# Hybrid attention trunk on one core: rotary embedding kept in PSUM, differential attention steps and a norm load moved, weight residuals emitted in pieces

## The chip, the cores and the metric

The kernel runs on one core of one Trainium2 chip. The time is the device time of one execution in microseconds, as the median of several runs. The core's engines are named as in the profile: PE is TensorE (PEld its weight loads), DVE is VectorE, ACT is ScalarE, POOL is GpSimd, and SP is SyncE, which here does nothing but issue DMAs.

## What is computed

Two layers over an input of 512 rows and 1024 columns, all in fp32. Each layer normalises its input, maps it by one input projection to three groups of heads, runs differential attention (a), stick-breaking attention (b) and forgetting attention (c), gates each with a SiLU path, maps the concatenation back, normalises and adds. Cut to what matters here:

```
h = rms_norm(x, g_pre)
qa, ka, va, ga, qs, ks, vs, gs, qf, kf, vf, gf, ff = split(h @ w_in)
qa, ka = rope(qa), rope(ka)              # first 16 of each 64 head dims
ya = rms_norm((softmax(q0 k0) - lam * softmax(q1 k1)) @ va, sub_gain) * silu(ga)
yb = stick_breaking(qs, ks, vs) * silu(gs)
yc = softmax(qf kf + forget bias) @ vf * silu(gf)
x  = x + rms_norm(concat(ya, yb, yc) @ w_out, g_post)
```

## The kernel before

Every operand of the projections is split in a high part (rounded to the matmul's type, `F32R`) and a low part (the rest), and `mm3` (L191 to L194) adds three matmuls per block: high x high, high x low, low x high.

Weights come in "halves" (`add_in_unit`, `add_out_unit`): tiles of 128 x 4 x 256 of `w_in`, or 128 x 2 x 512 of `w_out`. `load_to` (L162) issues the load of a half into one of three `raw` buffers on the SP queue. `split_to` (L170) makes the high part by a copy on ACT (L176), and the low part by subtractions of 256 columns on POOL (L182, four in a row for a half), or on DVE (L185) where the half is marked `lo="dve"` or in part `"both"`. Right after the split it issues the load of the third half ahead (L189), which needs the buffer of the half just split.

The order of all work is a plan. `do(cost, fn)` puts PE's projection work in a row and moves the plan's clock on; `at(t, fn)` puts other work at a time of that clock, in nanoseconds. At the end everything is sorted by that time and emitted (L850 to L852). Each engine runs its own instructions in that order, and an instruction that waits holds up all behind it on its engine. A tile's buffer is handed on when all that read it is done.

A half that is used at time t is split at t less its `lead` (2500 to 10833), and never later than the halves after it: `limit = min(limit, t - lead)` in L843 to L846.

One layer in the order of PE: values of group a, queries and keys of group a (four units of 256 columns for q and k, each of two projections of 24 matmuls of 512 columns), then values, queries and keys of group c, with the attention steps of group a between them, then group b with the steps of c, then the three gates with the steps of b, then the output projection in two passes of 512 columns. A projection's result lies in one of three PSUM buffers `pj` (L80).

The places that the change touches:
- `rope_stages` (L299): for each q and k projection of group a, DVE shuffles the result out of PSUM (L303, tile `sh`), multiplies it by the cosine table into an SBUF tile `ra` (L305), multiplies `sh` by the sine table (L306) and adds both into `ra` (L307). `qk_done` then makes high parts on ACT (L319) and low parts on DVE (L324) from `ra`; for groups b and c, which have no rope, from `pj` itself.
- `step_a` (L375): one step of differential attention (16 in a layer, a head and 128 queries each): two score matmuls into the two `s` buffers (L357), the masked minimum `mn` on DVE (L364), exponentials on ACT (L373), combination on DVE, transposes on PE, the product with the values (`av`, with the tile `on`, L402) and, 17029 after the step's start, `back` (L415). L629 places the steps: they start 3518 after the start of group c, over a span of 50075.
- `step_c`: `diag` (L456) on POOL adds the causal mask to the bias tile (`cm`) ahead of each score.
- The pre-norm of the next layer (L235 to L249): the mean and its power -0.5 stand on POOL (L242, L245), then DVE scales (L248) and PE transposes (L254).
- The output projection's first pass has six halves with low parts on POOL, the second six with low parts on DVE. At the end of the first pass DVE multiplies each accumulator by the post-norm gain (`y`, L756); the second pass takes over those `pj` buffers. `new_post` (L761) loads that gain, 9000 before the end of the first pass (L765).

Of the kernel before, what the change touches and what calls it, by code (L numbers as in the profile page):

```python
# [10 lines left out]
F32 = mybir.dt.float32  # L11
# [3 lines left out]
ALU = mybir.AluOpType  # L15
# [9 lines left out]
UW = 256  # L25
# [35 lines left out]
def hybrid_kernel(ctx, tc, x, w_in, forget_bias, diff_lambda, diff_subln, w_out, pre_norm, post_norm, consts, out):  # L61
    nc = tc.nc
# [26 lines left out]
    C = {}  # L89
# [30 lines left out]
    def t2(name, shape=None):  # L120
        return t2_p.tile(shape or [128, S], F32, name=name, tag="t2")
# [10 lines left out]
    now = [0.0]  # L132
# [5 lines left out]
    def at(t, fn):  # L138
        side.append((t, 0, len(side), fn))


    halves = []
    st_load = [0]
    st_split = [0]

    def add_in_unit(l, c0, extra=None):
        w = UW + (8 if extra is not None else 0)
        k0 = len(halves)
        for h in range(2):
            rows = w_in[l, h * 512:(h + 1) * 512]  # L150
            src = [(rows[:, c0:c0 + UW].rearrange("(k p) c -> p k c", p=128), 0, UW)]
            if extra is not None:
                src.append((rows[:, extra:extra + 8].rearrange("(k p) c -> p k c", p=128), UW, w))
            halves.append(dict(src=src, shape=[4, w], pool=whl_p, tag="whl", lead=9500 if h == 0 else 8000))
        return k0
# [6 lines left out]
    def load_to(k):  # L162
        while st_load[0] < min(k, len(halves)):
            h = halves[st_load[0]]
            h["raw"] = raw_p.tile([128] + h["shape"], F32, name="raw", tag="raw")
            for src, lo, hi in h["src"]:
                nc.sync.dma_start(out=h["raw"][:, :, lo:hi], in_=src)
            st_load[0] += 1

    def split_to(k):  # L170
        while st_split[0] < min(k, len(halves)):
            h = halves[st_split[0]]
            load_to(st_split[0] + 1)
            raw = h.pop("raw")
            hl = h["pool"].tile([128, 2] + h["shape"], F32R, name="hl", tag=h["tag"])
            nc.scalar.activation(out=hl[:, 0], in_=raw, func=AF.Copy)  # L176
            n = h["shape"][0]
            m = {"dve": 0, "both": n // 2}.get(h.get("lo"), n)
            for k in range(m):
                for c in range(0, h["shape"][1] // UW * UW, UW):  # L180
                    e = h["shape"][1] if c + 2 * UW > h["shape"][1] else c + UW
                    nc.gpsimd.tensor_tensor(out=hl[:, 1, k, c:e], in0=raw[:, k, c:e], in1=hl[:, 0, k, c:e].bitcast(F32),  # L182
                                            op=ALU.subtract)
            if m < n:
                nc.vector.tensor_tensor(out=hl[:, 1, m:n], in0=raw[:, m:n], in1=hl[:, 0, m:n].bitcast(F32),  # L185
                                        op=ALU.subtract)
            h["hl"] = hl
            st_split[0] += 1
            load_to(st_split[0] + 3)  # L189

    def mm3(ps, lh, ll, rh, rl, first, last):  # L191
        nc.tensor.matmul(out=ps, lhsT=lh, rhs=rh, start=first, stop=False)  # L192
# [106 lines left out]
    def rope_stages(st, scale):  # L299
        def turn():  # L300
            ps = st["ps"]
            sh = t2("sh")
            nc.vector.stream_shuffle(out=sh, in_=ps, mask=swap)  # L303
            ra = t2("ra")
            nc.vector.scalar_tensor_tensor(out=ra, in0=ps, scalar=scale, in1=C["rope"][:, 0], op0=ALU.mult, op1=ALU.mult)  # L305
            nc.vector.scalar_tensor_tensor(out=sh, in0=sh, scalar=scale, in1=C["rope"][:, 1], op0=ALU.mult, op1=ALU.mult)  # L306
            nc.vector.tensor_tensor(out=ra, in0=ra, in1=sh, op=ALU.add)  # L307
            st["ps"] = ra

        return [(0, turn)]  # L310

# [241 lines left out]
    def steps(fn, c, t0, span, w=W_STEP):  # L553
        t = t0
        for p in range(4):
            for i in range(NT):
                fn(t, c, p, i)
                t += span / 16 * w[i]
# [3 lines left out]
    def use(k, t):  # L562
        uses.append((k, t))
# [43 lines left out]
    def plan_layer(l, L):  # L607
# [9 lines left out]
        for g in ("a", "c", "b"):  # L617
            base = G[g]
            c = dict(pairs=[{} for _ in range(4)], lc=lc)
            st = {}  # L620
            c["v"] = lambda st=st: st["v"]
            c["o"] = lambda st=st: st["o"]
            c["cs"] = cs[l]
            t0 = now[0]
            at(t0, lambda st=st: st.update(v=v_p.tile([128, NT, 512], F32, name="v", tag="v")))
            if prev is not None:
                pst, pc, pg = prev
                at(t0, lambda pst=pst: pst.update(o=o_p.tile([128, 4, S], F32, name="o" + pg, tag="o")))
                steps(step_a if pg == "a" else step_c, pc, t0 + (3518 if pg == "a" else 3191), 50075 if pg == "a" else 46774)  # L629
            order = [(u, tt) for u in range(2) for tt in range(NT)]  # L630
            if g == "a":
                order = [(0, 0), (0, 1), (0, 2), (1, 0), (1, 1), (1, 2), (0, 3), (1, 3)]
            ks = []
            for u in range(2):
                ks.append(add_in_unit(l, base + 1024 + u * UW, 6144 if g == "a" and u == 0 else None))
            seen = set()
            for u, tt in order:
                ex = g == "a" and u == 0
                w = UW + (8 if ex else 0)
                if u not in seen:  # L640
                    seen.add(u)
                    use(ks[u], now[0])
                    use(ks[u] + 1, now[0] + 1300)
                    if g == "a" and u == 1:
                        halves[ks[u]]["lead"], halves[ks[u] + 1]["lead"] = 7500, 6500

                def done(pst, u=u, tt=tt, ex=ex, st=st, w=w):
                    def ev():
                        nc.scalar.activation(out=st["v"][:, tt, u * UW:(u + 1) * UW], in_=pst["ps"][:, 0:UW],
                                             func=AF.Copy)  # L650
                        if ex:
                            if "ff" not in ffd:
                                ffd["ff"] = lay.tile([128, 32], F32, name="ff", tag="ff")
                            nc.vector.tensor_copy(ffd["ff"][:, tt * 8:(tt + 1) * 8], pst["ps"][:, UW:w])
                    return [(0, ev)]
                proj_N(ks[u], w, tt, hT, done)
            if g == "a":
                at(now[0] + 2000, lambda: layer_consts(lcd, l))
                at(now[0] + 5000, lambda: ffd.update(lf=decay(ffd["ff"], lcd, l)))
                at(now[0] + 9000, lambda: decay_sum(ffd["lf"], l))  # L660
            sc = 0.125 if g == "b" else -0.125
            for u in range(2):
                for part in ("q", "k"):
                    k0 = add_in_unit(l, base + u * UW + (512 if part == "k" else 0))
                    use(k0, now[0])
                    use(k0 + 1, now[0] + 2600)
                    if g == "a" and u == 0 and part == "q":
                        for h in range(2):
                            halves[k0 + h].update(lead=2500, lo="both")
                    for cc in range(2):  # L670
                        keep = c["pairs"][2 * u + cc]
                        if part == "q":
                            proj_T(k0, cc, hT, lambda pst, keep=keep: qk_done(pst, g == "a", sc, keep, "q"))
                        else:
                            proj_T(k0, cc, hT, lambda pst, keep=keep: qk_done(pst, g == "a", 1.0, keep, "k"))
            prev = (st, c, g)
            ctxs[g] = (st, c)

        t0 = now[0]
# [55 lines left out]
        for u, (g, j0) in enumerate(order):  # L735
            k = add_out_unit(l, row[g] + j0, 0, whl_p, "whl")
# [24 lines left out]
        def new_post():  # L761
            t = qk_p.tile([128, 2, S], F32, name="gain", tag="qs")
            gains["post"] = [t[:, 0], t[:, 1]]
            load_gain(gains["post"], post_norm[l])
        at(now[0] - 9000, new_post)  # L765
        N = None
        if l + 1 < DEPTH:
            nx = {}
# [8 lines left out]
        for u, (g, j0) in enumerate(order):  # L777
            k = add_out_unit(l, row[g] + j0, 1, *((o_p, "o") if u < 3 else (v_p, "v") if u == 3 else (whl_p, "whl")))
# [3 lines left out]
        for tt in range(NT):  # L782
            sl = slice(tt * 128, (tt + 1) * 128)
            st = {}
# [54 lines left out]
    FIRST_LO = {0: "both", 1: "both"}  # L839
    first_norm(L)  # L840
    for l in range(DEPTH):
        L = plan_layer(l, L)
    limit = float("inf")  # L843
    for k, t in reversed(uses):
        limit = FIRST_SPLIT.get(k, min(limit, t - halves[k]["lead"]))
        at(limit, lambda k=k: split_to(k + 1))  # L846

    for k, e in FIRST_LO.items():
        halves[k]["lo"] = e
    with tc.manual_schedule():  # L850
        for _, _, _, fn in sorted(main + side, key=lambda e: e[:3]):
            fn()  # L852
# [28 lines left out]
```

## Time and profile before

| | us |
|---|---|
| time, median of 3 runs | 873.25 (873.04 to 873.48) |
| profiled execution | 873.66 |
| its span | 871.8 |
| PE busy | 854.9 |
| DVE, ACT, POOL busy | 495.3, 476.9, 449.6 |

The span runs from the first to the last instruction of the program on the core; the time of the execution has 1.9 us around it. The profile's rows tell for a group of equal instructions the busy time and the mean of one, and in a timeline the start, the length and, in brackets, for how long the engine stood idle before it and what ended that.

### The profile page before, as it was taken

To read this page: it belongs to the slowest core of one execution; us is meant where nothing else is said; L and a number is where in the kernel's file an instruction comes from. 1 tells how busy PE (TensorE), PEld (TensorE's weight loads), DVE (VectorE), ACT (ScalarE), POOL (GpSimd) and SP (SyncE) were. 2 spreads that over 40 slices of the span, in tenths; PEclk is the share of its full clock that TensorE was granted. 3 is DMA by queue.
4 is the path that set the end of the run, shared out by engine and by line. 5 is a ranking of instruction groups with operands and counts; after the bars stand their busy time and mean duration, and the time that the engine had idled before them with its cause. 6 is when DMAs were issued, how large, how long until landed. Compare 5 with 4: busy or idle time off the path is not lost.

```text
span 871.8 us, 13938 instructions
## 1 busy us (share of the span) xinstructions
PE 854.9 (98%) x4892; PEld 721.4 (83%) x4892; DVE 495.3 (57%) x1143; ACT 476.9 (55%) x1064; POOL 449.6 (52%) x680
## 2 busy tenths in 40 slices
PE   7999999999999999999999999999999999999997
PEld 5988998898778778777898889888987787877885
DVE  5378656544565778623563875664445476774322
ACT  4344667766776556633334356676667756664310
POOL 4366554655444548770364664555554544688301
PEclk9999999999999999999999999999999999999999
DMA  7365323432524221237264452325335422122522
GB/s 233 89 164 138 96 73 98 117 102 76 154 67 116 75 72 49 73 107 257 78 177 114 123 145 74 99 72 146 97 81 137 106 66 72 49 78 92 164 101 97
DMA packets 73207, 94.27 MB, mean 108 GB/s; under 512 B 6433, under 2 KB 56225, under 8 KB 73138
## 3 DMA queue, kind: packets, MB, share of 16 engines
q1 hardware_dynamic: 70834, 89.19, 35.6%
q10 hardware_dynamic: 2304, 4.20, 1.5%
q8 instruction: 39, 0.64, 0.3%
q14 instruction: 30, 0.25, 0.1%
HBM read 76.56 MB, written 4.23 MB: 93 GB/s over the span
## 4 chain that ended last, share of the span: by engine, by line
PE 78%; DVE 10%; ACT 4%; POOL 3%; issue 2%; DMA 2%; DVEq 0%; POOLq 0%; ACTq 0%; SPq 0%
PE pj L192 18%; PE pj L194 18%; PE pj L193 17%; PE s L339 6%; PE pt L347 5%; PE ov L437 4%; POOL hl L182 2%; PE acc L192 2%; PE acc L193 2%; PE acc L194 2%; PE ov L399 2%; DVE ra L307 2%; DVE sh L306 2%; DVE sh L303 1%; DVE qd L324 1%
## 5 line engine op out<-in xcount | busy, mean ns | idle before, releaser
L182 POOL TENSOR_TENSOR hl<-raw,hl 128x256 fp32r<-128x256 f32 (+1 forms) x420 | 343.5, 850 | 237.1 <-ACT hl L176 213.0
L192 PE MATMUL pj<-hT,hl 128*128 128x512 f32 x576 | 236.6, 411 | 0.0
L194 PE MATMUL pj<-hT,hl 128*128 128x512 f32 x576 | 225.7, 392 | 0.0
L193 PE MATMUL pj<-hT,hl 128*128 128x512 f32 x576 | 225.3, 391 | 0.0
L176 ACT ACTIVATE hl<-raw 128x1024 fp32r<-128x1024 f32 (+1 forms) x120 | 126.3, 1058 | 35.4 <-DMA raw<-in_w_out_dram 18.9
L194 PEld LDWEIGHTS pj<-hT,hl 128*128 128x128 f32 x576 | 108.1, 188 | 24.3
L192 PEld LDWEIGHTS pj<-hT,hl 128*128 128x128 f32 x576 | 108.4, 188 | 20.0 <-issue 2.1
L193 PEld LDWEIGHTS pj<-hT,hl 128*128 128x128 f32 x576 | 108.7, 189 | 16.9
L192 PE MATMUL pj<-hl,hT 128*128 128x256 f32 (+1 forms) x384 | 112.2, 292 | 0.3 <-ACT hT L257 0.2
L194 PE MATMUL pj<-hl,hT 128*128 128x256 f32 (+1 forms) x384 | 109.5, 285 | 0.5 <-DVE hT L258 0.5
L193 PE MATMUL pj<-hl,hT 128*128 128x256 f32 (+1 forms) x384 | 109.3, 285 | 0.5 <-POOL hl L182 0.5
L373 ACT ACTIVATE p<-p,mn 128x128 f32<-128x128 f32 (+3 forms) x128 | 71.1, 556 | 33.6 <-DVE mn L364 31.7
L506 DVE TENSOR_TENSOR_SCAN kp<-kp,c_masks 128x128 f32<-128x128 f32 (+3 forms) x64 | 67.2, 1051 | 18.3 <-ACT kp L499 17.8
L192 PEld LDWEIGHTS pj<-hl,hT 128*128 128x128 f32 x384 | 73.7, 192 | 1.3 <-ACT hT L257 1.0
L193 PEld LDWEIGHTS pj<-hl,hT 128*128 128x128 f32 x384 | 73.8, 192 | 1.2 <-POOL hl L182 0.7
L194 PEld LDWEIGHTS pj<-hl,hT 128*128 128x128 f32 x384 | 73.5, 191 | 1.2 <-DVE hT L258 1.2
L339 PE MATMUL s<-kd,qd 128*128 128x128 f32 (+1 forms) x192 | 62.6, 330 | 2.9 <-DVE mn L364 2.9
L350 ACT ACTIVATE pT<-pt 128x128 f32<-128x128 f32 (+3 forms) x96 | 41.2, 443 | 37.5 <-PE pt L347 37.2
L339 PE MATMUL s<-kd,qs 128*128 128x128 f32 (+1 forms) x192 | 61.2, 323 | 0.0
L511 DVE TENSOR_TENSOR sg<-sg,kp 128x127 f32<-128x127 f32 (+3 forms) x64 | 46.1, 721 | 5.5
L185 DVE TENSOR_TENSOR hl<-raw,hl 128x1024 fp32r<-128x1024 f32 (+2 forms) x18 | 21.0, 1175 | 44.8 <-ACT hl L176 44.7
L466 ACT ACTIVATE p<-p,rc 128x128 f32<-128x128 f32 (+3 forms) x64 | 35.0, 556 | 20.2 <-DVE rc L464 20.2
(142 smaller groups left out, 1453.0 us busy)
## 6 DMA issues: line engine op xcount, KB each, us to landing
raw<-in_w_in_dram SPq DMA_DIRECT2D x96, 512.0 KB, 3.7
qs<-qd SPq DMA_DIRECT2D x48, 256.0 KB, 4.5
raw<-in_w_out_dram SPq DMA_DIRECT2D x24, 512.0 KB, 3.6
cb<-cs ACTq DMA_DIRECT2D x16, 256.0 KB, 3.3
xl<-in_x_dram SPq DMA_DIRECT2D x4, 512.0 KB, 4.9
xt<-in_x_dram SPq DMA_DIRECT2D x8, 256.0 KB, 6.1
xs<-xt SPq DMA_DIRECT2D x8, 256.0 KB, 2.0
xt<-xs SPq DMA_DIRECT2D x8, 256.0 KB, 3.9
```

The costliest lines, as they stand in the source:

```text
L176: nc.scalar.activation(out=hl[:, 0], in_=raw, func=AF.Copy)
L182: nc.gpsimd.tensor_tensor(out=hl[:, 1, k, c:e], in0=raw[:, k, c:e], in1=hl[:, 0, k, c:e].bitcast(F32), op=ALU.subtract)
L192: nc.tensor.matmul(out=ps, lhsT=lh, rhs=rh, start=first, stop=False)
L193: nc.tensor.matmul(out=ps, lhsT=lh, rhs=rl, start=False, stop=False)
L194: nc.tensor.matmul(out=ps, lhsT=ll, rhs=rh, start=False, stop=last)
L339: nc.tensor.matmul(out=s[:, 0:n], lhsT=pr[q][:, m, i * 128:n], rhs=pr["k"][:, m, 0:n], start=(j == 0), stop=(j == 1))
L347: nc.tensor.transpose(out=pt[:, j * 128:(j + 1) * 128], in_=p[:, j * 128:(j + 1) * 128], identity=C["ident"])
L350: nc.scalar.activation(out=t, in_=src, func=AF.Copy)
L373: nc.scalar.activation(out=p[:, 0:n], in_=p[:, 0:n], func=AF.Exp, bias=st["mn", m], scale=-1.0, accum_out=su)
L466: nc.scalar.activation(out=p[:, 0:n], in_=p[:, 0:n], func=AF.Copy, scale=r)
L506: nc.vector.tensor_tensor_scan(out=rv, data0=rv, data1=C["first"][:, S - n:S][:, ::-1], initial=0.0, op0=ALU.mult, op1=ALU.max)
L511: nc.vector.tensor_tensor(out=sg[:, 0:n - 1], in0=sg[:, 0:n - 1], in1=kp[:, 1:n], op=ALU.mult)
```

## The change

- In `rope_stages` the tile `ra` is gone: L305 writes its product back into the PSUM tile, and L307 adds the sine part to it there. High and low parts of group a are then made from PSUM.
- The steps of differential attention start at 5000 instead of 3518 after group c's start, over 48600 instead of 50075.
- The post-norm gains are loaded 15000 instead of 9000 before the end of the first output pass.
- A half's POOL subtractions are no longer emitted at the split, but each as an item of the plan of its own (`low`), 1 after the split for the first and 700 later for each next one (all at once for the first four halves of the program). The load of the third half ahead goes out with the last of these pieces; for halves with all low parts on DVE still with the split.

```diff
+    def pieces(h):
+
+        n, w = h["shape"]
+        m = {"dve": 0, "both": n // 2}.get(h.get("lo"), n)
+        return [(k, c, w if c + 2 * UW > w else c + UW) for k in range(m) for c in range(0, w // UW * UW, UW)]
+
+    def low(k, i):
+        h = halves[k]
+        ps = pieces(h)
+        r, c, e = ps[i]
+        raw, hl = h["raw"], h["hl"]
+        nc.gpsimd.tensor_tensor(out=hl[:, 1, r, c:e], in0=raw[:, r, c:e], in1=hl[:, 0, r, c:e].bitcast(F32),
+                                op=ALU.subtract)
+        if i == len(ps) - 1:
+            load_to(k + 4)
+
     def split_to(k):
...
-            for k in range(m):
-                for c in range(0, h["shape"][1] // UW * UW, UW):
-                    e = h["shape"][1] if c + 2 * UW > h["shape"][1] else c + UW
-                    nc.gpsimd.tensor_tensor(out=hl[:, 1, k, c:e], in0=raw[:, k, c:e], in1=hl[:, 0, k, c:e].bitcast(F32),
-                                            op=ALU.subtract)
...
-            load_to(st_split[0] + 3)
+            if m == 0:
+                load_to(st_split[0] + 3)
...
-            ra = t2("ra")
-            nc.vector.scalar_tensor_tensor(out=ra, in0=ps, scalar=scale, in1=C["rope"][:, 0], op0=ALU.mult, op1=ALU.mult)
+            nc.vector.scalar_tensor_tensor(out=ps, in0=ps, scalar=scale, in1=C["rope"][:, 0], op0=ALU.mult, op1=ALU.mult)
             nc.vector.scalar_tensor_tensor(out=sh, in0=sh, scalar=scale, in1=C["rope"][:, 1], op0=ALU.mult, op1=ALU.mult)
-            nc.vector.tensor_tensor(out=ra, in0=ra, in1=sh, op=ALU.add)
-            st["ps"] = ra
+            nc.vector.tensor_tensor(out=ps, in0=ps, in1=sh, op=ALU.add)
...
-                steps(step_a if pg == "a" else step_c, pc, t0 + (3518 if pg == "a" else 3191), 50075 if pg == "a" else 46774)
+                steps(step_a if pg == "a" else step_c, pc, t0 + (5000 if pg == "a" else 3191), 48600 if pg == "a" else 46774)
...
-        at(now[0] - 9000, new_post)
+        at(now[0] - 15000, new_post)
...
     for k, t in reversed(uses):
         limit = FIRST_SPLIT.get(k, min(limit, t - halves[k]["lead"]))
         at(limit, lambda k=k: split_to(k + 1))
...
+        for i in range(len(pieces(halves[k]))):
+            at(limit + 1 + (700 * i if k > 3 else 0), lambda k=k, i=i: low(k, i))
```

## Rows read from the trace of the kernel before

**Rows 1.** The page: busy us (share of span) and instructions of each engine

```profile
PE 854.9 (98%) x4892; PEld 721.4 (83%) x4892; DVE 495.3 (57%) x1143; ACT 476.9 (55%) x1064; POOL 449.6 (52%) x680
```

**Rows 2.** Waits of PE: waiter, releaser: us in total, times, longest us

```profile
PE s L339 <- DVE mn L364: 2.9, 4, 1.1
...
PE pj L192 <- DVE y L756: 1.0, 1, 1.0
```

**Rows 3.** Timeline of PE at its waits: start, length, instruction, idle before

```profile
93.24 0.39 PE L339 MATMUL s<-kd,qd 128*128 128x256 f32 x1 [1.09 <-DVE mn L364]
...
225.25 0.39 PE L339 MATMUL s<-kd,qd 128*128 128x256 f32 x1 [0.37 <-DVE mn L364]
...
405.21 0.39 PE L193 MATMUL acc<-hl,yq 128*128 128x512 f32 x1
405.44 0.39 PE L194 MATMUL acc<-hl,yq 128*128 128x512 f32 x1
406.81 0.50 PE L192 MATMUL pj<-hl,yv 128*128 128x512 f32 x1 [0.98 <-DVE y L756]
...
442.28 0.63 PE L254 MATMUL pt<-c_masks,xn 128*128 128x128 f32 x4 [0.66 <-DVE xn L248]
```

**Rows 4.** Groups by line and form: count | busy, mean ns | idle before

```profile
L324 DVE SCALAR_TENSOR_TENSOR kd<-pj,kd 64x512 fp32r<-64x512 f32 x32 | 22.0, 689 | 11.9 <-ACT kd L319 11.5
...
L307 DVE TENSOR_TENSOR ra<-ra,sh 128x512 f32<-128x512 f32 x16 | 17.0, 1060 | 0.5
...
L306 DVE SCALAR_TENSOR_TENSOR sh<-sh,rope 128x512 f32<-128x512 f32 x16 | 15.6, 972 | 0.0
...
L324 DVE SCALAR_TENSOR_TENSOR kd<-ra,kd 64x512 fp32r<-64x512 f32 x16 | 11.0, 686 | 5.8 <-ACT kd L319 5.6
L305 DVE SCALAR_TENSOR_TENSOR ra<-pj,rope 128x512 f32<-128x512 f32 x16 | 11.0, 685 | 0.4
...
L720 ACT ACTIVATE pj<-pj 128x512 f32<-128x512 f32 x16 | 9.7, 608 | 7.7 <-DVE oc L717 7.7
...
L720 ACT ACTIVATE gs<-pj 128x512 f32<-128x512 f32 x8 | 4.9, 610 | 0.0
```

**Rows 5.** Timelines of PE and DVE around the eighth rope of layer 0

```profile
84.35 0.28 PE L192 MATMUL pj<-hl,hT 128*128 128x256 f32 x1
...
90.50 0.33 PE L192 MATMUL pj<-hl,hT 128*128 128x256 f32 x1
...
87.17 0.74 DVE L303 STREAM_SHUFFLE sh<-pj 128x512 f32<-128x512 f32 x1
...
91.45 1.40 DVE L324 SCALAR_TENSOR_TENSOR kd<-ra,kd 64x512 fp32r<-64x512 f32 x2 [0.70 <-ACT kd L319]
```

**Rows 6.** Timelines of POOL and DVE ahead of the wait at 225 us

```profile
221.63 2.81 POOL L182 TENSOR_TENSOR hl<-raw,hl 128x256 fp32r<-128x256 f32 x4 [1.31 <-ACT hl L176]
...
224.90 0.29 DVE L364 CUSTOM_DVE_ANT_0 p<-s,cm 128x128 f32<-128x128 f32 x1 [0.36 <-POOL cm L456]
```

**Rows 7.** Timelines of POOL and DVE ahead of the wait at 442 us

```profile
436.48 3.99 POOL L182 TENSOR_TENSOR hl<-raw,hl 128x264 fp32r<-128x264 f32 x4 [1.29 <-ACT hl L176]
...
430.21 2.40 DVE L248 SCALAR_TENSOR_TENSOR xn<-xt,rpre,gain 128x512 f32<-128x512 f32 x2 [1.11 <-POOL rpre L245]
...
441.38 1.42 DVE L248 SCALAR_TENSOR_TENSOR xn<-xt,rpre,gain 128x512 f32<-128x512 f32 x2 [2.24 <-POOL rpre L245]
```

**Rows 8.** Timelines of POOL and SP (DMA issues) between the output passes

```profile
385.38 4.79 POOL L182 TENSOR_TENSOR hl<-raw,hl 128x256 fp32r<-128x256 f32 x4 [2.61 <-ACT hl L176]
...
390.20 6.51 SPq L167 DMA_DIRECT2D raw<-in_w_out_dram  x4
```

**Rows 9.** Timelines of SP and DVE: post-norm gains in layers 0 and 1

```profile
400.30 1.29 SPq L294 DMA_DIRECT2D gain<-in_post_norm_dram  x2
...
406.06 2.48 DVE L756 TENSOR_TENSOR y<-acc,gain 128x512 f32<-128x512 f32 x4 [3.80 <-DMA gain<-in_post_norm_dram]
...
823.67 1.21 SPq L294 DMA_DIRECT2D gain<-in_post_norm_dram  x2
```

More of the change, by code (lines that the diff above doesn't have):

```diff
@@ L173, in split_to @@
             load_to(st_split[0] + 1)
-            raw = h.pop("raw")
+            raw = h["raw"]
             hl = h["pool"].tile([128, 2] + h["shape"], F32R, name="hl", tag=h["tag"])
@@ L843, in hybrid_kernel @@
     limit = float("inf")
+    for k, e in FIRST_LO.items():
+        halves[k]["lo"] = e
     for k, t in reversed(uses):
@@ L846, in hybrid_kernel @@
         at(limit, lambda k=k: split_to(k + 1))
-    for k, e in FIRST_LO.items():
-        halves[k]["lo"] = e
+        for i in range(len(pieces(halves[k]))):
+            at(limit + 1 + (700 * i if k > 3 else 0), lambda k=k, i=i: low(k, i))
     with tc.manual_schedule():
```

## The prediction

> **What bounds the kernel now.** I read the busy times first: TensorE (PE) is busy 98% of the span [rows 1], so only time in which PE waits can be won, and all else is cover. Next the view of PE's waits: apart from the first 25 us it names the s tiles of the attention scores, waiting for VectorE's (DVE's) masked minimum `mn`, and the second half of the output projection, waiting for the product `y` [rows 2]. Then I found each wait in PE's timeline [rows 3]. Ends of matmuls are modelled: a 512-column matmul is shown with 0.39 us but the next starts 0.23 us after it, so each idle time shown hides 0.39 - 0.23 = 0.16 us more. The four places are:
> - 93.24 us, L339, 1.09 + 0.16 = 1.25 us;
> - 225.25 us, L339, 0.37 + 0.16 = 0.53 us;
> - 406.81 us, L192, 0.98 + 0.16 = 1.14 us;
> - 442.28 us, L254, 0.66 + 0.16 = 0.82 us.
> The list of waits has four for L339, 2.9 us in total [rows 2]: that is 1.09 and 0.37 twice, once in each layer. The third and fourth stand in layer 0 alone. All together 2 x 1.25 + 2 x 0.53 + 1.14 + 0.82 = 5.5 us. That is the most the change can win.
>
> **Rope in PSUM, and the later differential steps.** PE waits at 93.24 because DVE comes late: `mn` of the first scores queues behind the rope and the low parts of the eighth q/k projection, whose L324 ends at 91.45 + 1.40 = 92.85 [rows 3, 5]. That projection ended on PE at 84.35, where the first matmul of group c's values starts, and its shuffle started only at 87.17: DVE is 2.8 us behind [rows 5]. The price per rope is in the rows by form [rows 4]: L305, which reads PSUM and one SBUF operand, 0.685 us; L306 and L307, which read two SBUF operands, 0.97 and 1.06 in the mean. The change gives L307 the form of L305 (its first input is `ps` in PSUM), so it should fall by 1.06 - 0.685 = 0.37, and I take 0.42 for a slow one. L306 still reads `sh` and the table from SBUF and stays. Shuffle and L305 keep their inputs. The low parts L324 move their source from SBUF to PSUM: 0.686 against 0.688 us, nothing.
>
> What no row shows is a DVE write into PSUM. The nearest row is ScalarE's (ACT's) sigmoid in place in PSUM, 0.608 against 0.610 us into SBUF [rows 4]; the upper bound is the slowest form of the same size, 1.06 [rows 4]; below 0.685 I expect nothing, as no row of 512 columns there is shorter. I take 0.685, by the in-place row.
>
> So by the eighth projection some six earlier ropes give back 0.42 each, 2.5 us: its shuffle starts near 87.17 - 2.5 = 84.7, just after PE has done, and its low parts end at 92.85 - 2.5 - 0.42 = 89.9. The scores are put 1.48 us later in plan time, so the first falls behind the second value tile and the `mn` finds DVE free. I cost the wait of 1.25 us at zero, in both layers: **2.50 us** won.
>
> What is late next: the pj buffer. Until now it was free after L305; now it is held until L324 ends. There are three; group c's third value tile takes that of the eighth projection, and starts at 90.50 [rows 5], in the changed order about 90.3. The buffer is free at 89.9: a cover of 0.4 us. With an extra e per rope it is 8e later, so PE would wait 8e - 0.4 us in each layer, from e = 0.05 us on. [...]
>
> The steps of differential attention are also 3% closer. DVE already waits there for `back` (L415) before it may overwrite `on`, and these waits grow by a fraction of a projection quarter. PE waits nowhere there, as all its waits for `mn` are placed above [rows 2], so I cost it at zero, with up to 0.3 us per layer if a score waits.
>
> **Low parts piece by piece.** Work and engine stay (L182 on GpSimd, POOL); four pieces in a row now let other POOL work between them, when the plan time of that work falls among them.
> - 225.25: POOL ran four pieces from 221.63 to 224.44, then the `cm` for which DVE idled 0.36 us until 224.90 [rows 6]. By the plan times (pieces at 25609, 26309, 27009, 27709 of group b, the second diag at 26362) it now goes behind two pieces of 0.70 us and is done by about 223.6. DVE could not start `mn` before 224.54, as 224.90 less the 0.36 idle. I win 0.36 of 0.53, twice: **0.7 us**.
> - 442.28: the pre-norm's mean and power waited for four pieces, 436.48 to 440.47; xn follows at 441.38 [rows 7]. Plan times: pieces at -6699, -5999, -5299, the mean at -5276, the last at -4599. So it goes ahead of one piece, worth 1.0 us; but that piece then runs beside L248, which takes 1.20 each beside pieces and 0.71 alone [rows 7]. xn is ready 1.0 - 0.5 = 0.5 earlier at the least; I take **0.4 us** of 0.82.
> - The raw loads are issued by the last piece, not at the split. They wait for that piece anyway, so SP is blocked less; what passes them (qs copies, xs stores) gains, without being on the path.
> - One place gets worse. The last half of the first output pass has its due time cut to that of the first half of the second pass (-20833), 368 ns behind the one before it (-21201). Their pieces now interleave: three pieces of the earlier half sit behind the later half's first, which starts at 385.38 [rows 8]. Four pieces took 4.79 us there, 2.0 over 4 x 0.70, beside two low parts on DVE; now one of these is left there, so the sixth piece, the earlier half's last, ends near 385.38 + 6 x 0.70 + 1.0 = 390.6. PE wants that half from 405.67 - 2 x 24 x 0.23 = 394.6 on (24 matmuls for each of two halves), so this is covered. But its raw buffer is what the next load waits for, and SP holds two loads behind that one. The run of four loads that took 6.51 us from 390.20 [rows 8] starts near 390.6 and has one load more, 6.51 / 4 = 1.6 us: it ends about 2.0 us later, in both layers.
>
> **The post-norm load.** In layer 0 the products at 406.06 waited 3.80 us for gains issued at 400.30, 5.7 us earlier; in layer 1 the issue at 823.67 made no wait, having no loads of a next layer ahead of it [rows 9]. Moved 6 us of plan time ahead, it passes two such loads, and goes right behind the last load of the second pass. That was over at 396.7 [rows 8]; with the 2.0 us above it is 398.7, so landing near 404.4, and `y` from 404.4 to 405.1. PE wants the buffer at 405.44 + 0.23 = 405.67 [rows 3]. I cost the wait at zero and win **1.1 us** in layer 0; the cover is 0.5 us, in layer 1 too, which needed none before. Both ends: zero, or 1.14 us in each layer. The next layer's loads get two issues of 0.6 us ahead of them, and are split after the second pass has begun: nothing. The new qs buffer was last used by attention that is long over.
>
> **Sum.** 2.50 + 0.7 + 0.4 + 1.1 = 4.7 us. The profiled execution took 873.66 us (span 871.8, 1.9 around it): 868.96. The median is 0.41 us below the profiled one; I carry that over: 873.25 - 4.7 = 868.6 us (rounded).
>
> **The rivals.**
> - PSUM costs DVE more than the rows say (e = 0.2 us per rope, about half of the bound 0.37): PE waits 8 x 0.2 - 0.4 = 1.2 us per layer at the third value tile: 868.6 + 2.4 = 871.0. [...] Against it: the equal rows of L324. Chance 0.10.
> - The gains come late after all: the interleaved halves delay the loads by well over 2.5 us, layer 0 keeps 1.14 us while layer 1 gets as much: 868.6 + 2.3 = 870.9. For it: the cover of 0.5 us rests on a chain of estimated steps. Chance 0.14.
> - The pieces change nothing for those who wait (POOL's neighbours come ready later than I think): 868.6 + 1.1 = 869.7. Chance 0.10.
> - Slower: a DVE write into PSUM goes at 1.06 us, for L305 and L307, e = 0.74. The eighth low part would end at 89.9 + 5.9 = 95.8, PE waits 5.5 us in each layer in place of 1.25: 868.6 + 11 = about 880. It gets slower than before from e = 0.34 on, where 8e - 0.4 = 2.35 us per layer eats the whole 4.7. Against it: the in-place row of ACT. Chance 0.05.
> - The change does not do what it says and the waits only move along (DVE late for another reason, another POOL neighbour): 873. Chance 0.05.
> - The forecast, 868.6, with 867.6 to 869.6 for it alone: 0.56.
>
> **How the numbers follow.** At the low end all of the 5.5 us go and some contention with them: 867.4. At the high end the first two rivals, 871.0, and a little: 871.3. Outside lie the two rivals of 0.05 and some of the tails. A measurement of this kernel can tell 0.2%, 1.7 us, from no change: faster is below 871.5, which holds forecast and three rivals, 0.90, less their tails: 0.88; the same 0.07; slower 0.05.
>
> **What would show it.** Right: L307 near 0.69 us, no idle time over 0.2 us before L339 at the start of the differential steps; no wait before L192 of the second pass in either layer; L339 near 225 waiting under 0.25 us. Wrong: PE waiting at a value tile's first matmul for DVE L324 (first and fourth rival); `y` waiting for the gains (second); `mn` still idle for `cm` (third).

## The result, and the profile after

The changed kernel takes 882.8 us (median of 4 runs, 879.59 to 884.42) against 873.3 before: a ratio of 1.0104, with a 95% interval of 1.0074 to 1.0135. The forecast was 868.6 us. The change makes the kernel 9.5 us slower where 4.7 us had been expected off it. The profiled execution took 881.96 us with a span of 879.8, 8.0 more than before. In three of the experiments below one execution ran slow (e3 3522.74, e5 940.96, e8 1207.43 us); it is counted in the median given, but not in the range and the ratio.

Line numbers of the changed kernel differ: the three matmuls L192 to L194 are now L204 to L206, the low parts on POOL L181, those on DVE L196, the weights' high parts on ACT L192, the rope's sum L318, high and low parts of queries and keys L329 and L334, the product `y` L766, the copy of values out of PSUM L659.

The page of the changed kernel, its busy line, answers [rows 1]:

```profile
PE 857.9 (98%) x4892; PEld 722.4 (82%) x4892; DVE 487.9 (55%) x1143; ACT 475.1 (54%) x1064; POOL 441.3 (50%) x680
```

DVE and POOL have 7 to 8 us less to do, and the span is longer all the same. PE shows 3 us more of busy time for the same 4892 instructions; 1.8 us of that come back below, under the clock, and the rest is not taken apart. The view of PE's waits (us in total, times, longest), to be held against [rows 2]:

```profile
PE pj L204 <- DVE y L766: 3.3, 2, 2.1
PE pj L204 <- DVE kd L334: 3.2, 2, 1.6
PE pj L204 <- ACT v L659: 2.9, 2, 1.5
...
PE pt L357 <- ACT wT L360: 0.5, 2, 0.2
```

The waits for `mn` are gone, as forecast. Two others of about the same place have come, for the low parts L334 and for the values' copy L659, and the wait for `y` is in both layers. PE's timeline at the start of group c and around `y`, changed kernel, layers 0 and 1:

```profile
87.05 0.28 PE L206 MATMUL pj<-hl,hT 128*128 128x256 f32 x1
88.95 0.39 PE L204 MATMUL pj<-hl,hT 128*128 128x256 f32 x1 [1.62 <-DVE kd L334]
...
93.72 0.39 PE L204 MATMUL pj<-hl,hT 128*128 128x256 f32 x1 [1.45 <-ACT v L659]
...
409.08 0.50 PE L204 MATMUL pj<-hl,yv 128*128 128x512 f32 x1 [1.22 <-DVE y L766]
...
443.50 0.39 PE L206 MATMUL pj<-hl,yq 128*128 128x512 f32 x1
444.32 0.63 PE L266 MATMUL pt<-c_masks,xn 128*128 128x128 f32 x4 [0.43 <-DVE xn L260]
...
838.92 0.50 PE L204 MATMUL pj<-hl,yv 128*128 128x512 f32 x1 [2.06 <-DVE y L766]
```

With the 0.16 us that the modelled ends hide, the second and third value tile now wait 1.78 and 1.61 us, together 3.39 us, in place of 1.25 [rows 3]; the same two waits stand in layer 1. Now the account of the span. The starts of like matmuls in the two traces give the shifts: value tiles 2 x (3.39 - 1.25) = +4.3; the steps of differential attention, closer together, some +0.9; `y` +0.2 in layer 0 (1.38 for 1.14) and +2.2 in layer 1 (none before); a stretch behind the wait in layer 1 at a granted clock of 0.57 in the mean +1.8; the waits near 225 us gone, 2 x -0.6; that at 442 us shorter, -0.2. Together +8.0 us, the difference of the spans.

**Where the value tiles wait.** DVE's timeline at the seventh and eighth rope of layer 0, changed kernel, and ACT's beside it:

```profile
85.55 0.70 DVE L318 TENSOR_TENSOR pj<-pj,sh 128x512 f32<-128x512 f32 x1
87.51 1.39 DVE L334 SCALAR_TENSOR_TENSOR kd<-pj,kd 64x512 fp32r<-64x512 f32 x2 [1.26 <-ACT kd L329]
...
91.33 0.70 DVE L318 TENSOR_TENSOR pj<-pj,sh 128x512 f32<-128x512 f32 x1
93.29 1.39 DVE L334 SCALAR_TENSOR_TENSOR kd<-pj,kd 64x512 fp32r<-64x512 f32 x2 [1.26 <-ACT kd L329]
```

```profile
92.06 1.19 ACT L329 ACTIVATE kd<-pj 64x512 fp32r<-64x512 f32 x2 [3.51 <-DVE pj L318]
93.28 0.38 ACT L659 ACTIVATE v<-pj 128x256 f32<-128x256 f32 x1
```

The sum writes into PSUM in 0.70 us, as forecast. But the low parts, which began 0.70 us after the sum [rows 5], now begin 1.26 us after it: when both of ACT's copies (92.06 + 1.19 = 93.25) are done and not only the first. In the kernel before, where copies and low parts read the SBUF tile `ra`, ACT's two copies at this place run to 92.06, and the low part starts at 91.45 [rows 5], beside the second copy:

```profile
90.78 1.28 ACT L319 ACTIVATE kd<-ra 64x512 fp32r<-64x512 f32 x2 [3.23 <-DVE ra L307]
```

A rope takes 5.78 us from one to the next (87.51 to 93.29). The buffer of the seventh projection is free only with the end of its low parts at 88.90, and PE's second value tile starts at 88.95. ACT's copies of the eighth are late with DVE, the values' copy L659 stands behind them, and the third value tile waits for that: it starts at 93.72, when the first of these copies is done (93.28 + 0.38) and a buffer is free, and before the eighth projection's low parts end (93.29 + 1.39 = 94.68).

**Where `y` waits.** DVE's timeline, changed kernel, ahead of `y` in both layers, then SP's in layers 0 and 1, and ACT's in layer 1:

```profile
407.20 1.23 DVE L196 TENSOR_TENSOR hl<-raw,hl 128x1024 fp32r<-128x1024 f32 x1 [2.36 <-ACT hl L192]
408.34 2.48 DVE L766 TENSOR_TENSOR y<-acc,gain 128x512 f32<-128x512 f32 x4
...
837.04 1.23 DVE L196 TENSOR_TENSOR hl<-raw,hl 128x1024 fp32r<-128x1024 f32 x1 [3.48 <-ACT hl L192]
838.18 2.47 DVE L766 TENSOR_TENSOR y<-acc,gain 128x512 f32<-128x512 f32 x4
```

```profile
392.67 9.93 SPq L167 DMA_DIRECT2D raw<-in_w_out_dram  x5
402.65 0.93 SPq L306 DMA_DIRECT2D gain<-in_post_norm_dram  x2
...
810.89 18.94 SPq L167 DMA_DIRECT2D raw<-in_w_out_dram  x6
```

```profile
835.95 1.06 ACT L192 ACTIVATE hl<-raw 128x1024 fp32r<-128x1024 f32 x1 [3.64 <-DMA raw<-in_w_out_dram]
```

`y` does not wait for its gains any more. It stands behind a low part of the output weights on DVE, L196, the last of the second pass; that waits for ACT's high part, and that for its load. In layer 1 SP had issued this load by 829.83 (810.89 + 18.94), and ACT could begin at 835.95, 6.1 us later.

### The profile page after: what moved, and what is told of

It is laid out like the page before. It is cut to its first block, busy times and chain, and to the rows that moved or that the text cites. A ratio compares the mean times of both kernels' runs of the same rounds, so it can differ in the third digit from the quotient of the medians.

```text
span 879.8 us, 13942 instructions
## 1 busy us (share of the span) xinstructions
PE 857.9 (98%) x4892; PEld 722.4 (82%) x4892; DVE 487.9 (55%) x1143; ACT 475.1 (54%) x1064; POOL 441.3 (50%) x680
## 5 line engine op out<-in xcount | busy, mean ns | idle before, releaser
L181 POOL TENSOR_TENSOR hl<-raw,hl 128x256 fp32r<-128x256 f32 (+1 forms) x420 | 337.0, 828 | 248.5 <-ACT hl L192 223.9
L204 PE MATMUL pj<-hT,hl 128*128 128x512 f32 x576 | 237.2, 412 | 0.0
L206 PE MATMUL pj<-hT,hl 128*128 128x512 f32 x576 | 225.8, 392 | 0.0
L192 ACT ACTIVATE hl<-raw 128x1024 fp32r<-128x1024 f32 (+1 forms) x120 | 126.3, 1057 | 44.1 <-DMA raw<-in_w_out_dram 27.7
L206 PEld LDWEIGHTS pj<-hT,hl 128*128 128x128 f32 x576 | 108.1, 188 | 24.2
L204 PEld LDWEIGHTS pj<-hT,hl 128*128 128x128 f32 x576 | 108.4, 188 | 20.0 <-issue 2.1
L204 PE MATMUL pj<-hl,hT 128*128 128x256 f32 (+1 forms) x384 | 112.7, 293 | 6.4 <-DVE kd L334 3.2
L206 PE MATMUL pj<-hl,hT 128*128 128x256 f32 (+1 forms) x384 | 109.7, 286 | 0.5 <-DVE hT L270 0.5
L204 PEld LDWEIGHTS pj<-hl,hT 128*128 128x128 f32 x384 | 73.9, 193 | 8.1 <-DVE kd L334 3.6
L206 PEld LDWEIGHTS pj<-hl,hT 128*128 128x128 f32 x384 | 73.7, 192 | 1.2 <-DVE hT L270 1.2
L196 DVE TENSOR_TENSOR hl<-raw,hl 128x1024 fp32r<-128x1024 f32 (+2 forms) x18 | 20.1, 1116 | 54.7 <-ACT hl L192 54.7
L329 ACT ACTIVATE kd<-pj 64x512 fp32r<-64x512 f32 x48 | 28.3, 589 | 36.7 <-DVE pj L318 28.2
```

Of the source, the lines that this page charges most:

```text
L181: nc.gpsimd.tensor_tensor(out=hl[:, 1, r, c:e], in0=raw[:, r, c:e], in1=hl[:, 0, r, c:e].bitcast(F32), op=ALU.subtract)
L206: nc.tensor.matmul(out=ps, lhsT=ll, rhs=rh, start=False, stop=last)
L329: nc.scalar.activation(out=d[H[m], m], in_=st["ps"][H[m]], func=AF.Copy, scale=sc)
```

## The experiments

All are timed against the kernel before. In the order of what they tell:

| | us, median | lowest to highest | ratio to before, 95% |
|---|---|---|---|
| the change | 882.8 | 879.6 to 884.4 | 1.0074 to 1.0135 |
| e1 rope undone | 873.01 | 870.8 to 875.6 | 0.9986 to 1.0007 |
| e2 pieces kept together | 876.81 | 876.3 to 877.3 | 1.0025 to 1.0053 |
| e3 sum to SBUF | 871.99 | 870.7 to 875.4 | 0.9974 to 0.9997 |
| e4 = e2 + e3 | 869.40 | 869.3 to 869.5 | 0.994 to 0.997 |
| e5 only the rope | 876.78 | 876.5 to 876.9 | 1.0022 to 1.0048 |
| e6 only the pieces | 877.64 | 876.3 to 879.8 | 1.0036 to 1.006 |
| e7 only the steps | 872.76 | 872.5 to 873.2 | 0.9983 to 1.0 |
| e8 only the post-norm load | 872.58 | 872.4 to 873.3 | 0.9981 to 0.9998 |
| e10 copies by turns | 883.66 | 880.2 to 886.6 | 1.006 to 1.0147 |
| e11 = e4, steps over 50075 | 868.46 | 868.4 to 868.5 | 0.9927 to 0.9958 |

**e1, the rope undone.** All of the change but the rope, which goes through `ra` in SBUF as before.

```diff
-            nc.vector.scalar_tensor_tensor(out=ps, in0=ps, scalar=scale, in1=C["rope"][:, 0], op0=ALU.mult, op1=ALU.mult)
+            ra = t2("ra")
+            nc.vector.scalar_tensor_tensor(out=ra, in0=ps, scalar=scale, in1=C["rope"][:, 0], op0=ALU.mult, op1=ALU.mult)
...
-            nc.vector.tensor_tensor(out=ps, in0=ps, in1=sh, op=ALU.add)
+            nc.vector.tensor_tensor(out=ra, in0=ra, in1=sh, op=ALU.add)
+            st["ps"] = ra
```

> The changed kernel with rope back in the SBUF tile ra; its three other parts stay. Theory R (rope): with its operand in PSUM the first low part waits until both high-part copies are done (DVE idles 1.26 us before L334, 0.70 before), a rope takes DVE 5.81 us for PE's 5.44 per projection, and the pj buffer is held as long; so PE waits 1.78 and 1.62 us at the second and third value tile of group c in each layer. Then both waits go: 6.8 us less than the changed kernel, about 875.5. Rival S (steps): the waits come from the later and closer differential steps: within 1 us of the changed kernel. Both leave the waits for y (1.4 and 2.2 us) as they are.

Measured 873.01 us, 2.5 us below the figure expected. PE's waits in the profiled execution, which with 875.58 us was the slowest of the ten:

```profile
PE pj L204 <- DVE y L768: 3.4, 2, 2.3
```

No value tile waits, so these waits belong to the rope in PSUM. The rest of the change, which should have won 2 us and more, is no faster than before: what is left in this execution is the wait for `y`, 2.45 us in layer 0 and 1.22 in layer 1; its mean granted clock, 0.997, is the lowest of the ten (0.998 and 0.999 in the others). The median, 2.6 us lower, likely has less of that wait.

**e2, the pieces of a half kept together** where they would reach past the split of the next half; all else as in the change. The two halves between the output passes then no longer interleave.

```diff
+        room = limit
         limit = FIRST_SPLIT.get(k, min(limit, t - halves[k]["lead"]))
         at(limit, lambda k=k: split_to(k + 1))
-        for i in range(len(pieces(halves[k]))):
-            at(limit + 1 + (700 * i if k > 3 else 0), lambda k=k, i=i: low(k, i))
+        n = len(pieces(halves[k]))
+        gap = 700 if k > 3 and limit + 1 + 700 * (n - 1) < room else 0
+        for i in range(n):
+            at(limit + 1 + gap * i, lambda k=k, i=i: low(k, i))
```

> The changed kernel, but a half's pieces are emitted at once where their spread would run into the next split (the last two halves of the first output pass). Theory P (interleaving): two halves' pieces interleave there, the raw loads behind them come late, so DVE makes the last low part of the second pass late and y stands behind it: the PE waits of 1.4 us (layer 0) and 2.2 us (layer 1) go, and with the latter the stretch of 3.4 us at the lower clock, 5 us in all: about 877.5. Rival G (gains): the post-norm load moved ahead slows the last weight load by sharing the DMA engines: the waits stay within 0.5 us. Both leave the value tiles' waits as they are.

Measured 876.81 us, as expected. DVE's timeline shows `y` waiting for something of its own again, the squares on ACT, and PE's waits have no `y`; those of the value tiles stay:

```profile
406.80 2.73 DVE L766 TENSOR_TENSOR y<-acc,gain 128x512 f32<-128x512 f32 x4 [2.00 <-ACT sq L765]
```

```profile
PE pj L204 <- DVE kd L334: 3.3, 2, 1.7
PE pj L204 <- ACT v L659: 2.9, 2, 1.5
```

So the interleaved halves are what makes `y` late. The runs also lie within about 1 us, where those of kernels with the interleaved halves lie 3.5 to 6.4 us apart.

**e3, the sum to SBUF.** The cosine product stays in PSUM in place, and only the sum goes to `ra`, so that it still has one PSUM operand, while high and low parts read SBUF.

```diff
-            nc.vector.tensor_tensor(out=ps, in0=ps, in1=sh, op=ALU.add)
+            ra = t2("ra")
+            nc.vector.tensor_tensor(out=ra, in0=ps, in1=sh, op=ALU.add)
+            st["ps"] = ra
```

> The changed kernel, with the cosine product still written back to PSUM but the sum (L318) written to an SBUF tile, from which high and low parts are made. Theory R: L318 keeps its 0.70 us, the first low part waits for one copy only (0.70 us again), a rope takes DVE about 5.2 us, pj is free after the sum; no wait at the value tiles, 6.8 us less than the changed kernel: about 875.5. If instead writing to PSUM were what costs (the cosine product), half of the waits or more would stay: 879 or above. Rival S as for the first kernel: no change.

Measured 871.99 us, 3.5 us below the figure expected: I had put too much on `y` here as well (its profiled execution, with 870.71 us the fastest, has one such wait, of 0.8 us). DVE's groups by form, and its timeline at the eighth rope:

```profile
L319 DVE TENSOR_TENSOR ra<-pj,sh 128x512 f32<-128x512 f32 x16 | 11.1, 691 | 0.5
L336 DVE SCALAR_TENSOR_TENSOR kd<-ra,kd 64x512 fp32r<-64x512 f32 x16 | 11.0, 686 | 5.8 <-ACT kd L331 5.6
```

```profile
83.21 1.41 DVE L336 SCALAR_TENSOR_TENSOR kd<-ra,kd 64x512 fp32r<-64x512 f32 x2 [0.70 <-ACT kd L331]
...
88.40 1.40 DVE L336 SCALAR_TENSOR_TENSOR kd<-ra,kd 64x512 fp32r<-64x512 f32 x2 [0.70 <-ACT kd L331]
90.39 0.29 DVE L376 CUSTOM_DVE_ANT_0 p<-s,c_masks 128x128 f32<-128x128 f32 x1 [0.59 <-PE s L351]
```

This is the rope that I had forecast: 5.19 us from one to the next, the low parts done at 89.80 (forecast 89.9), and `mn` finds DVE idle. The one difference to the change is where the sum lies; the rope is 5.78 - 5.19 = 0.59 us longer when the copies and the low parts read it from PSUM, and none of that is in the operations (0.686 us each here, 0.689 in the change).

**e4, both remedies**, e2 and e3 in one kernel.

> Both remedies: the sum in SBUF, and the pieces kept together where they would cross. Theories R and P together: the forecast's mechanism as it was meant, all of 6.8 and 5 us less than the changed kernel: about 870, below the kernel before by 3 us or more. If the two are not independent (one wait only taking over when the other goes), 873 or above.

Measured 869.4 us, faster than the kernel before. With the pieces kept together, the rope in PSUM costs e2 - e4 = 7.4 us. The interleaving costs 2.6 us here (e3 - e4), and 6.0 us in the change (change - e2); why it costs less without the rope in PSUM is not taken apart. SP's timeline shows the run of loads as it was before [rows 8], and the gains right behind it:

```profile
388.78 6.37 SPq L167 DMA_DIRECT2D raw<-in_w_out_dram  x4
395.20 0.93 SPq L306 DMA_DIRECT2D gain<-in_post_norm_dram  x2
```

**e5 to e8, each part alone** on the kernel before, with the lines of the change's diff.

> The kernel before with the rope sum in PSUM and nothing else of the change. Theory R (a low part whose source is in PSUM waits until both high copies are made, so a rope takes DVE 5.8 us and PE's projections 5.44): DVE's idle time before the low parts of group a is 1.26 us per pair instead of 0.70, PE waits at the start of group c some 3.4 us or more per layer in place of 1.25 us, time 877 to 880 us, about 878. Rival S (the rope alone is harmless and costs only together with the later steps, which hold the third value tile): 871.5 to 873.5 us.

e5: 876.78 us, a little below its range, but slower than before. PE waits 3.3 us in two places for the low parts (L322 there) and 2.5 for the values' copy. The rope is harmful by itself; the later steps are not needed for it.

> The kernel before with the low parts in pieces and nothing else. Theory T (interleaved halves delay the run of loads by 2 us, so that the gains and the last low part on DVE come later for y): the waits near 225 go (0.6 us each) and that at 442 by 0.2, y waits some 3 us in layer 0 (gains, which are still loaded late) and 2.2 us in layer 1, perhaps with 1.8 us at half clock behind one of them: 875 to 878 us. Rival: the pieces by themselves cost nothing and give 1.4 us: 871.9 us.

e6: 877.64 us, as expected. The gains are still loaded late here, so `y` waits for them in layer 0, and in layer 1 there is a wait of 1.8 us for `y`, where 2.2 had been expected; the waits near 225 us are down by 0.6 each. PE's timeline, and then PE busy, PEld, DVE, ACT, POOL, granted clock, DMA share and GB/s behind that wait:

```profile
408.12 0.50 PE L204 MATMUL pj<-hl,yv 128*128 128x512 f32 x1 [3.00 <-DVE y L768]
```

```profile
407.90:411.30 3.40, 3.18 (x9) 2.55 (x10) 1.96 (x4) 0.00 (x0) 0.00 (x0) 0.66 1.01 293
```

> The kernel before with the differential steps moved and nothing else. Theory: the wait for mn of 1.25 us per layer goes, since the first score comes 1.5 us later and behind the second value tile, and a wait of 0.4 us per layer for the transposed weights (PE behind ACT) comes with the closer steps: 873.3 - 2.5 + 0.8 = 871.6 us. Rival (DVE is 2.8 us behind, so the score still waits for mn): 872.5 to 873.5 us, with the wait for mn still seen.

e7: 872.76 us, in the rival's range, but without the rival's sign. The wait for `mn` of 1.25 us is gone in both layers, though DVE is as late as before: the second of the two `s` buffers and the value tile behind the first score cover it. But two thirds of that are lost again in the steps of differential attention: held against the kernel before, PE's matmuls behind the steps are only 0.4 us earlier per layer than those ahead of them, where 1.25 us could have been won.

> The kernel before with the load of post-norm gains moved and nothing else. Theory: the wait before y in layer 0 goes, 1.1 us, and nothing comes in layer 1: 872.2 us. Rival (the last low part on DVE is right behind, with its load pushed back by the gains, or the load of a next layer's weights is late): 873 us or more, with a wait left before y.

e8: 872.58 us. The wait before `y` is gone, and held against the kernel before, PE's matmuls behind it are earlier by 1.25 us more than those ahead of it; the median is 0.8 us lower.

The four alone come to 3.4 + 4.3 - 0.6 - 0.8 = +6.3 us, the change to +9.5. Part of the rest is that rope and steps remove the same wait for `mn`, 2.5 us, which can be won only once. What the remaining bit hangs on I have not taken apart.

**e10, high and low parts by turns.** In the change both copies are emitted on ACT and then both low parts on DVE; here a copy and its low part, twice.

```diff
             for m in range(2):
                 nc.scalar.activation(out=d[H[m], m], in_=st["ps"][H[m]], func=AF.Copy, scale=sc)
+                nc.vector.scalar_tensor_tensor(out=d[H[1 - m], m], in0=st["ps"][H[m]], scalar=sc,
+                                               in1=d[H[m], m].bitcast(F32), op0=ALU.mult, op1=ALU.subtract)
```

> The changed kernel, but for group a a high copy and its low part are emitted by turns (high, low, high, low) instead of both copies and then both low parts. Theory R (the operations that two engines do on one PSUM tile go one after the other in the order in which they are emitted): the first low part waits for its own copy alone, 0.70 us as from SBUF, but now the second copy on ACT waits for that low part (ACT idle about 0.7 us or more between the two), and the second low part for that copy, so DVE stands idle a second time and nothing is won: a rope still takes DVE 5.8 us or more, time 881 to 885 us. Rival (what made the low part late is that a copy out of PSUM or its hand-over is slow): the two copies run one right behind the other as before, DVE's idle time per pair is 0.70 and the rope 5.2 us, time 875 to 878 us.

Measured 883.66 us, as the first theory had it. ACT's and DVE's timelines at the eighth rope:

```profile
92.54 0.59 ACT L345 ACTIVATE kd<-pj 64x512 fp32r<-64x512 f32 x1 [2.83 <-DVE pj L318]
93.89 0.59 ACT L345 ACTIVATE kd<-pj 64x512 fp32r<-64x512 f32 x1 [0.75 <-DVE kd L346]
```

```profile
93.17 0.69 DVE L346 SCALAR_TENSOR_TENSOR kd<-pj,kd 64x512 fp32r<-64x512 f32 x1 [0.66 <-ACT kd L345]
94.51 0.69 DVE L346 SCALAR_TENSOR_TENSOR kd<-pj,kd 64x512 fp32r<-64x512 f32 x1 [0.66 <-ACT kd L345]
```

The first low part now starts 0.66 us after the sum, but the second copy waits for it, though it reads the other 64 partitions and needs nothing of it. Reads of one PSUM tile by ACT and DVE go one after the other here, in the order of emission. The traces of the kernels before and after show the same throughout: out of PSUM no copy (64 in the kernel before, 96 in the changed one) runs at the same time as a low part, while out of SBUF the first low part and the second copy overlap by 0.62 us in each of the 16 ropes of the kernel before; in e3, too, the low part starts 0.70 us after the sum at the eighth rope, as in the kernel before. The tile that both write, `qd` or `kd`, is the same in either case, so it is not what parts them. The wait is one between instructions of the program (ACT's idle 0.75 us ends with DVE's L346); whether the halves could be read side by side was not tried.

**e11, the best version:** e4 with the steps over 50075 instead of 48600.

```diff
-                steps(step_a if pg == "a" else step_c, pc, t0 + (5000 if pg == "a" else 3191), 48600 if pg == "a" else 46774)
+                steps(step_a if pg == "a" else step_c, pc, t0 + (5000 if pg == "a" else 3191), 50075 if pg == "a" else 46774)
```

> The kernel of e4 (sum in SBUF, crossing pieces kept together) with the differential steps over 50075 instead of 48600, starting at 5000. If the closer steps are what makes PE wait twice 0.4 us for the transposed weights: 868.6 us. Rival (the wait stays or moves to the end of the group): 869.2 us or more.

Measured 868.46 us. Held against the kernel before, PE's matmuls behind the steps of differential attention are earlier by 1.3 us per layer more than those ahead of them, the whole wait for `mn`, where e4 had 0.84; and the wait for the transposed weights is gone. It is 4.8 us faster than the kernel before.

## Why the prediction was wrong

Its account of the kernel before held: the four places where PE waits were the right ones. In e11 all that is left of them is 0.6 us at the next layer's norm, and it takes 868.46 us where 868.6 was forecast. That the two agree to 0.1 us is in part luck: in e11's trace the four places give about 5.2 us for the 4.7 of the forecast. The change itself does two things that the prediction had costed at nothing. By the medians, the 14.2 us between forecast and measurement are 7.4 for the rope in PSUM (e2 - e4), 6.0 for the interleaved halves (the change - e2) and 0.9 for the closer steps (e4 - e11). The fourth rival's figure, about 880, lies near the result by luck: the write into PSUM that it priced at 1.06 us took 0.70.

- **The step that failed first: "The low parts L324 move their source from SBUF to PSUM: 0.686 against 0.688 us, nothing."** The durations are right (0.689), the wait ahead of them is not. I priced the operation and did not price the hand-over: from PSUM the low part starts after both copies (1.26 us), from SBUF after its own (0.70). The rows were there. ACT and DVE of the kernel before, low parts of a group without rope, whose source is in PSUM already:

```profile
221.46 1.18 ACT L319 ACTIVATE qd<-pj 64x512 fp32r<-64x512 f32 x2
```

```profile
222.67 1.41 DVE L324 SCALAR_TENSOR_TENSOR qd<-pj,qd 64x512 fp32r<-64x512 f32 x2 [2.02 <-ACT qd L319]
```

  The low part starts with the end of both copies, 222.64. In the groups by form the idle time is 11.9 us for 16 pairs from PSUM and 5.8 for 8 from SBUF [rows 4], the same mean, as DVE had other work in part of the wait: a mean of idle time does not tell how long a hand-over takes.
- **The cover of 0.4 us and the rule 8e - 0.4** held in kind. With e = 0.59 they give 4.3 us per layer; measured 3.39. The prediction had the third value tile waiting, for the eighth projection's low parts; it was the second, for those of the seventh (1.78 us), and then the third, for the values' copy behind ACT's late copies (1.61 us). The prediction had "slower from e = 0.34 on" and the right sign, a value tile's first matmul waiting for low parts, but looked for e in the write into PSUM. That write is as cheap as it said (0.70 us), and so the rivals were dismissed by the rows of the wrong operation: the sign listed for the first and the fourth came true without their cause. No run shows the first rival's 0.2 us per rope as a price of PSUM in the operations: the low parts took 0.689 us from PSUM against 0.686 from SBUF, and the 0.59 us that came instead lies in the wait ahead of them.
- **The interleaved halves** were seen, with the right delay at first: loads from 390.6, and with group c 2.07 us late, 392.67. Then the sizes fail: I took 1.6 us for one load more, 8.1 in all, and the run took 9.93, as each of the last two loads waits for a buffer that the split of a late load must free.
- **The post-norm load: "`y` from 404.4 to 405.1"** counted the gains as the last to come. They were on time. I left out that DVE takes its instructions in order (in layer 1 ACT is done with the first accumulator at 837.49, but `y` starts at 838.18, behind L196 of 837.04), and that the last low part of the second pass stands ahead of `y`; the load of that part is the last of the delayed run. I had checked the loads of the next layer, not those of this one. The rival "gains late after all" has the cause (the interleaving), but names the wrong transfer and has less than half of the price: 2.3 us for 6.0. Alone, on the loads as they were, the move is worth about what it said: e8.
- **The clock** was in no case. It costs 1.8 us in layer 1 (below).
- **The steps**, costed at zero with up to 0.3 us per layer: 0.41 us at one wait for the transposed weights and small gaps besides, 0.4 to 0.5 us per layer by e11. Mis-sized.
- **Low parts in pieces, at 225:** right, and more: 0.6 us in each layer for 0.36. **At 442:** 0.23 us for 0.4. The third rival falls.

## What to carry to other kernels

Before an intermediate result moves from SBUF to PSUM, look up who reads it beside the engine that makes it: here ACT's copies and DVE's low parts, side by side on an SBUF tile, went one after the other on a PSUM tile, and eight times 0.59 us ate a cover of 0.4. Price the start of an operation from the row where the same hand-over stands in a timeline, not from the group's duration. And when pieces of two weight tiles may cross, follow the delayed buffer to the last load of the run and to every instruction queued behind its split, not only to the transfer that the change moves.

## What the runs showed of the hardware

In the changed kernel the granted clock fell from 1.00 to 0.50 behind PE's wait in layer 1, and the work behind the wait was slower. Windows of the changed kernel behind the `y` of layer 1 (start:end, length, PE, PEld, DVE, ACT, POOL busy with counts, granted clock, DMA share, GB/s), and PE's timeline there:

```profile
836.00:838.90 2.90, 0.86 (x4) 0.38 (x2) 1.86 (x3) 2.90 (x8) 0.92 (x3) 1.00 0.37 126
838.90:842.30 3.40, 3.38 (x9) 2.64 (x10) 1.75 (x3) 0.41 (x2) 0.30 (x2) 0.57 0.42 143
```

```profile
840.42 0.63 PE L205 MATMUL pj<-hl,yq 128*128 128x512 f32 x1
840.85 0.63 PE L206 MATMUL pj<-hl,yq 128*128 128x512 f32 x1
...
843.62 0.40 PE L205 MATMUL pj<-hl,yq 128*128 128x512 f32 x1
843.86 0.39 PE L206 MATMUL pj<-hl,yq 128*128 128x512 f32 x1
```

PE had stood idle for 2.06 us by the trace; over the 3.4 us that follow the granted clock is 0.57 in the mean, 0.91 up to 839.5 and 0.50 from there on, and matmuls start 0.43 us apart instead of 0.24. That costs 1.8 us on top of the wait, nearly as much again. e6 shows the same behind its wait of 3.00 us (0.66 in the window above). Behind the waits of 1.62, 1.45 and 1.22 us in the changed kernel the granted clock stayed at 1.0.

A load of one output half (512 KB) took 3.6 us from issue to landing in the median of the changed kernel, but 6.1 us from SP's issue to ACT's start for the last of the delayed run in layer 1, with the gains and four loads of `xt` issued right behind it. The runs do not settle which execution gets the longer landings. That they are why kernels with the interleaved halves vary by 3.5 to 6.4 us from one execution to the next, and e2, e4 and e11 by about 1 us or less, is likely but not shown, since one execution of each kernel was profiled.
